# Two trunk layers on one core: layer norm in place without GpSimd, region A four units at a time, residual outputs behind later evictions

## The chip, the cores and the metric

The kernel runs on one core of one Trainium2 chip. The metric is device microseconds of a whole execution: the median of three runs before the change is 1775.16 us (1774.89 to 1776.41). The profiled execution is one more run of the same kernel; every duration below is from it.

## The reference, cut to what matters

```python
def layer(x, cond, lp, layer_idx, ctx_cache):
    sh1, sc1, g1, sh2, sc2, g2 = ...          # from silu(cond) @ w_ada + b_ada
    y, new_ctx = mixers(x * (1.0 + sc1) + sh1, lp, ...)   # w_in, conv | diff attention | MLA, w_out
    x = layer_norm(DEEPNORM_ALPHA * x + g1 * y, lp["ln1_g"], lp["ln1_b"])
    hf = x * (1.0 + sc2) + sh2
    f = (silu(hf @ lp["w_ff1"]) * (hf @ lp["w_ff3"])) @ lp["w_ff2"]
    x = layer_norm(DEEPNORM_ALPHA * x + g2 * f, lp["ln2_g"], lp["ln2_b"])
    return x, new_ctx
```

Two layers, width 1024, for 512 sample tokens and 128 prompt tokens; everything in float32, and the prompt has its own modulation vector. `layer_norm` subtracts the mean over the 1024 features, divides by the deviation, then applies a gain and a shift.

## The kernel before

**Layout.** Activations lie feature by feature: `x[k]`, k = 0 to 7, has 128 features on the partitions and 640 tokens in the columns. The columns form region A (0 to 383: 256 sample and the 128 prompt tokens) and region B (384 to 639). Every product is made as three reduced-precision products of a high and a low half (hi·hi, hi·lo, lo·hi), so the input `h[k]` of a stage is a pair (hi, lo), and a weight block ("unit", 128 output features, 1024 inputs) is DMAed to `stg` (three buffers), cast by ACT (`wu` hi, L142) and subtracted by DVE (`wu` lo, L144) into one of four `wu` buffers. PSUM tiles `mm` are two banks wide, three of them.

**Stages of a layer.** Input projections (`stage_in`), attention, output projection with first residual and norm (`stage_residual`, call it norm 1), feed-forward (`stage_ff`), whose f2 part ends in norm 2. The three norms with work behind them are norm 1 of layer 0, norm 2 of layer 0 and norm 1 of layer 1; the last norm has code of its own (`ln_last`), which stays.

**The seam of a norm.** A norm needs the sums of all eight feature tiles, so the kernel splits tokens by region: the last four output tiles of the residual stage are made for region B first and then for region A, and while region A's are made, B's norm runs; then the first four units of the next stage are multiplied for region B, while A's norm runs, and last for region A. `ln_steps` returns the steps: `stats` (matmuls of the sums with ones, then on [128, 3] tiles mean, variance and a Newton iteration for 1/deviation `ny`, L321 to 335, and `nb` = -mean·`ny`, L747), `spread` (PE transposes that spread `ny` over the partitions into `tr`, `nb` into `ac`, L753), and eight `normal(k)`: DVE a = x·G·`tr` (L767), ACT z = `ac`·G + B (L769), a += z (L770, DVE, or POOL for two tiles of region B), ACT casts h hi (L638), and lo = a - hi on DVE for region A, on POOL for region B (L639). After the last, ACT copies `ac` and `tr` to `accQ`, `accS` (L778, L779). The residual stream itself is normalised later by eight `output(k)`: three POOL operations on x (L786 to 788), then for norm 2 a DMA `xd<-x` that spills the tile (L642). `output` waits for no engine but POOL's own earlier work.

**What sets the order.** `jobs2` multiplies two units for one region and calls `hook()` after each k and unit; the tables `NEXT_FF` and `NEXT_IN` say after which hook (of 32 in region B) the next step of A's norm is issued. A scheduler then orders each engine by its own timeline; `behind(ins)` pins an instruction after another. `urgent` pins the products behind the norm's own matmuls. `PIN` keeps DVE from starting tile k before tile k - 3 is done.

**Layer 1's input stage.** After its first four units (ax0, ac0, ab0, ax1 in region order) come dk0, dq0, dk1, dq1, dv and others. dk0 and dq0 are evicted by ACT (L905, L918), rotated (DVE shuffle L826, POOL L827 for q, DVE L828, L829), split into hi and lo, moved by DMA to `ddk` and `ddq` in DRAM and loaded back as `dkp` and `dqp`; the first score matmul (L1192) needs them. The convolution of layer 1 has its first term on POOL (`cv`, L884) and the rest on DVE (L885 to 888).

Of the kernel before, what the change touches and what calls it, by code (L numbers as in the profile page):

```python
# [192 lines left out]
class Trunk:  # L193
    def __init__(self, ctx, tc, a, o):
# [160 lines left out]
    def jobs2(self, us, x, reg, nk, hooks=()):  # L355

        nc = self.nc
        c0, c1 = REG[reg]
        out = [self.mm()[:, 128:768] for _ in us]
        for k in range(nk):  # L360
            for u, ps in zip(us, out):
                for i, (pw, px) in enumerate(((0, 0), (0, 1), (1, 0))):
                    with self.behind(self.urgent):
                        self.last = nc.tensor.matmul(ps[:, c0:c1], u[:, pw, 128 * k:128 * k + 128], x(k, px)[:, c0:c1],  # L364
                                                     start=(k == 0 and i == 0), stop=(k == nk - 1 and i == 2)).ins
                self.hook()
        return out
# [311 lines left out]
    def ln_stats(self, reg, p):  # L679
# [4 lines left out]
        for i, j in enumerate(tl):  # L684
            nc.tensor.matmul(p[:, 4 * i:4 * i + 2], self.accS[:, 128 * j:128 * j + 128], self.ones2,
                             start=True, stop=True)
            self.urgent = nc.tensor.matmul(p[:, 4 * i + 2:4 * i + 4], self.accQ[:, 128 * j:128 * j + 128], self.ones2,
                                           start=True, stop=True).ins
# [47 lines left out]
    def ln_steps(self, l, s, reg):  # L736
# [4 lines left out]
        st, shift, scale, p = [], self.accQ, self.accS, self.spare  # L741

        def stats():
            y, mean = self.ln_stats(reg, p)
            nb = self.small(3, "nb")
            nt = len(TILES[reg])
            self.newton_end = nc.vector.scalar_tensor_tensor(nb[:, :nt], mean, -1.0, y[:, :nt], ALU.mult, ALU.mult).ins  # L747
            st.extend((y, nb))
# [12 lines left out]
        def normal(k):
            a, z = self.tmp("a", 1), self.tmp("z", 3)
            gb = self.gb[l + s]
            for g, b0, b1 in [(0, c0, min(c1, 256)), (1, 256, 384)] if reg == "A" else [(0, c0, c1)]:
# [1 line left out]
                with self.behind(pins.get(k - PIN)):
                    nc.vector.scalar_tensor_tensor(a[:, b0:b1], self.x[k][:, b0:b1], G, st[2][:, b0 - c0:b1 - c0],  # L767
                                                   ALU.mult, ALU.mult)
                nc.scalar.activation(z[:, b0:b1], st[3][:, b0 - c0:b1 - c0], AF.Identity, scale=G, bias=B)  # L769
            add = (nc.gpsimd if k in add_on else nc.vector).tensor_add(a[:, c0:c1], a[:, c0:c1], z[:, c0:c1]).ins  # L770
            lo = self.split_h(k, a, reg, nc.gpsimd if k in lo_on else nc.vector)
            self.pool_end = lo if k in lo_on else add if k in add_on else self.pool_end
            if PINLO and k not in lo_on:
                pins[k] = lo
            elif k not in add_on:
                pins[k] = add
            if k == NK - 1:
                nc.scalar.copy(shift[:, c0:c1], st[3])  # L778
                nc.scalar.copy(scale[:, c0:c1], st[2])  # L779
# [67 lines left out]
    def in_evac(self, l, n, ps, regs):  # L847
# [42 lines left out]
        elif n[:3] == "ckv" or n[:2] == "cq":  # L890
            raw, sq = self.t(name="raw"), self.t(name="sqr")
            nc.scalar.copy(raw, ps)
            nc.scalar.activation(sq, raw, AF.Square)
# [142 lines left out]
    def stage_in(self, l):  # L1036
# [28 lines left out]
        else:  # L1065
            us = [self.W.get((n, l)) for n in names[:nskew]]
            for regs in "BA":
                if regs == "B":
                    self.window(NEXT_IN)
                for i in range(0, nskew, 2):  # L1070
                    for n, ps in zip(names[i:i + 2], self.jobs2(us[i:i + 2], h, regs, NK)):
                        self.in_evac(l, n, ps, regs)
                        if regs == "A":
                            self.W.done()
                            self.tick()
                self.ln_inputs()
            self.ln_outputs(0 if OUTR else 1 << 30)
# [633 lines left out]
```

## Time and profile before

| | us |
|---|---|
| median of three runs | 1775.16 |
| the profiled execution's own time | 1775.88 |
| its span, first to last instruction | 1774.1 |
| PE matmul busy | 1702.8 (96%) |
| DVE busy | 1021.1 (58%) |
| ACT busy | 590.6 (33%) |
| POOL busy | 420.0 (24%) |
| mean granted TensorE clock | 0.98 of full speed |

[...] All stretches below are in us from the start of the span.

### The profile page before, as it was taken

To read this page: it belongs to the slowest core of one execution; us is meant where nothing else is said; L and a number is where in the kernel's file an instruction comes from. 1 tells how busy PE (TensorE), PEld (TensorE's weight loads), DVE (VectorE), ACT (ScalarE), POOL (GpSimd) and SP (SyncE) were. 2 spreads that over 40 slices of the span, in tenths; PEclk is the share of its full clock that TensorE was granted. 3 is DMA by queue.
4 is the path that set the end of the run, shared out by engine and by line. 5 is a ranking of instruction groups with operands and counts; after the bars stand their busy time and mean duration, and the time that the engine had idled before them with its cause. 6 is when DMAs were issued, how large, how long until landed. Compare 5 with 4: busy or idle time off the path is not lost. (4 is left out here: it accounts for less than half of the span.)

```text
span 1774.1 us, 29684 instructions
## 1 busy us (share of the span) xinstructions
PE 1702.8 (96%) x11983; PEld 1593.7 (90%) x11983; DVE 1021.1 (58%) x1824; ACT 590.6 (33%) x1010; POOL 420.0 (24%) x400
## 2 busy tenths in 40 slices
PE   8999989998999999999999899899989999999997
PEld 6998867698999999999989798677989999999997
DVE  3656776759566566856397558764682332232236
ACT  1334545525321121122243436554442212211221
POOL 0011113447701010110377111233582000000014
PEclk9999989999999999999989899899999999999998
DMA  9564584321355444544314544722122222222211
GB/s 333 196 204 140 168 250 145 109 90 48 101 149 150 149 136 140 174 130 150 93 51 166 170 113 149 210 64 84 48 75 81 72 75 81 64 79 84 68 53 59
DMA packets 100872, 217.38 MB, mean 123 GB/s; under 512 B 12160, under 2 KB 28928, under 8 KB 100736
## 3 DMA queue, kind: packets, MB, share of 16 engines
q1 hardware_dynamic: 100736, 215.50, 39.3%
q8 instruction: 94, 1.54, 0.4%
q14 instruction: 42, 0.34, 0.1%
HBM read 185.28 MB, written 30.18 MB: 121 GB/s over the span
## 5 line engine op out<-in xcount | busy, mean ns | idle before, releaser
L343 PE MATMUL mm<-h,wu 128*128 128x384 f32 (+1 forms) x4944 | 735.9, 310 | 0.2
L343 PEld LDWEIGHTS mm<-h,wu 128*128 128x128 f32 x4944 | 724.9, 189 | 6.9 <-issue 5.3
L142 ACT CAST wu<-stg 128x1024 fp32r<-128x1024 f32 (+2 forms) x200 | 201.5, 1011 | 701.3 <-issue 347.1
L144 DVE TENSOR_TENSOR wu<-stg,wu 128x1024 fp32r<-128x1024 f32 (+2 forms) x200 | 246.0, 1234 | 145.6 <-ACT wu L142 143.9
L343 PE MATMUL mm<-gh,wu 128*128 128x256 f32 (+1 forms) x1184 | 258.8, 310 | 0.0
L343 PEld LDWEIGHTS mm<-gh,wu 128*128 128x128 f32 x1184 | 198.7, 188 | 0.9 <-issue 0.6
L343 PE MATMUL mm<-gl,wu 128*128 128x384 f32 (+1 forms) x592 | 182.8, 309 | 0.0
L1196 DVE TENSOR_REDUCE nm<-mm 128x1 f32<-128x640 f32 x128 | 104.7, 818 | 54.7 <-PE mm L1192 53.8
L1545 DVE TENSOR_TENSOR gs<-gs,mm 128x640 f32<-128x640 f32 (+2 forms) x48 | 36.6, 763 | 152.7 <-PE mm L343 147.6
L653 DVE SCALAR_TENSOR_TENSOR x<-mm,ga,x 128x512 f32<-128x512 f32 x48 | 35.9, 749 | 146.2 <-PE mm L343 146.2
L672 POOL TENSOR_TENSOR accS<-x 128x640 f32<-128x640 f32 x4 | 10.0, 2490 | 443.6 <-DVE x L659 418.5
L343 PEld LDWEIGHTS mm<-gl,wu 128*128 128x128 f32 x592 | 111.4, 188 | 0.2 <-issue 0.2
L512 DVE SCALAR_TENSOR_TENSOR acc<-rawt,scT,acc 128x512 f32<-128x512 f32 x98 | 75.8, 773 | 57.8 <-DMA rawt<-in_w_ada 56.1
L364 PE MATMUL mm<-h,wu 128*128 128x384 f32 (+1 forms) x576 | 95.6, 329 | 1.0 <-DVE v L694 0.5
L364 PEld LDWEIGHTS mm<-h,wu 128*128 128x128 f32 x576 | 91.5, 206 | 3.3 <-issue 0.8
L343 PE MATMUL mm<-hi,wu 128*128 128x384 f32 (+1 forms) x400 | 89.8, 311 | 0.1
L510 POOL TENSOR_SCALAR acc<-rawt,scT 128x512 f32<-128x512 f32 x14 | 9.8, 701 | 313.0 <-PE tr L527 312.9
L1192 PE MATMUL mm<-mk,mq 96*128 96x384 f32 (+1 forms) x384 | 75.3, 337 | 5.8 <-ACT P L1207 2.3
L517 DVE SCALAR_TENSOR_TENSOR rawt<-rawt,scT 128x512 f32<-128x512 f32 x98 | 74.7, 763 | 2.1 <-POOL rawt L510 2.1
L1192 PEld LDWEIGHTS mm<-mk,mq 96*128 96x128 f32 x384 | 64.1, 201 | 12.7 <-ACT P L1207 4.9
L343 PEld LDWEIGHTS mm<-hi,wu 128*128 128x128 f32 x400 | 68.0, 188 | 2.6 <-issue 1.5
L1207 ACT ACTIVATE P<-mm,nm 128x640 f32<-128x640 f32 x56 | 44.6, 797 | 57.3 <-DVE nm L1196 45.0
(279 smaller groups left out, 2446.8 us busy)
## 6 DMA issues: line engine op xcount, KB each, us to landing
stg<-in_w_ff SPq DMA_DIRECT2D x104, 512.0 KB, 3.6
rawt<-in_w_ada SPq DMA_DIRECT2D x160, 256.0 KB, 3.0
stg<-in_w_in SPq DMA_DIRECT2D x30, 512.0 KB, 4.4
stg<-in_w_ff SPq DMA_DIRECT2D x32, 448.0 KB, 3.3
raw<-in_w_ada SPq DMA_DIRECT2D x32, 256.0 KB, 6.2
stg<-in_w_out SPq DMA_DIRECT2D x16, 512.0 KB, 4.3
mk<-kd SPq DMA_DIRECT2D x32, 240.0 KB, 5.8
mq<-qd SPq DMA_DIRECT2D x32, 192.0 KB, 5.5
```

The source lines that it names most:

```text
L142: nc.scalar.copy(u[:, 0, :ncol], t[:, :ncol])
L144: (nc.gpsimd if self.lo_pool else nc.vector).tensor_sub(u[:, 1, :ncol], t[:, :ncol], u[:, 0, :ncol].bitcast(F32))
L343: self.last = nc.tensor.matmul(out, w(k, pw), x(k, px), start=(k == 0 and i == 0), stop=(k == nk - 1 and i == 2)).ins
L364: self.last = nc.tensor.matmul(ps[:, c0:c1], u[:, pw, 128 * k:128 * k + 128], x(k, px)[:, c0:c1], start=(k == 0 and i == 0), stop=(k == nk ...
L512: nc.vector.scalar_tensor_tensor(self.acc[0], w, c[0], self.acc[0], ALU.mult, ALU.add)
L517: nc.vector.scalar_tensor_tensor(self.acc[1], w, c[1], self.acc[1], ALU.mult, ALU.add)
L653: nc.vector.scalar_tensor_tensor(lat(x), lat(ps), ga[:, 0, s, m:m + 1], lat(x), ALU.mult, ALU.add)
L672: nc.gpsimd.tensor_add(self.accS[:, c0:c1], self.first[0][:, c0:c1], x[:, c0:c1])
L1192: nc.tensor.matmul(ps[:, 128 + c0:128 + c1], q[:96, qc:qc + 128], k[:96, c0:c1], start=(i == 0), stop=(i == len(pairs) - 1))
L1196: nc.vector.tensor_reduce(nm, s, axis=AX.X, op=ALU.max, negate=True)
L1207: self.exp_end = nc.scalar.activation(P, s, AF.Exp, bias=nm, accum_out=sm).ins
L1545: nc.vector.tensor_mul(gs[:, c0:c1], gs[:, c0:c1], ps[:, c0:c1])
```

## The change

- `ln_steps`: `nb` goes, the mean itself is spread (into `ac`, as soon as it is there), then `ny`. `normal(k)` works in place: DVE x -= mean (L776 of the changed kernel), DVE x *= `ny` (L777), both with one operand in PSUM; ACT hv = G·x + B (L781, in region A in two pieces), ACT cast hi (L782), DVE lo = hv - hi (L783) for both regions. `PIN` is 2. The copies of `ac` and `tr` go.
- `output(k)` is one ACT instruction per tile and region, x = g·x + b (L790), pinned behind `out_pin`, which is set at a later eviction; three are issued per feed-forward unit pair (`OUTR`), four per unit of the input stage (`OUTI`). The spills follow.
- `jobs_by_tile` replaces `jobs2`: the two units of a pair lie in two banks of one `mm` tile; in region A all four units run at once, tile k by tile k (12 matmuls per k) for k = 0 to 5, then unit by unit for k = 6, 7 (`ENDS`). The four `wu` buffers come free only there. `hook()` is called once per k, so region B has 16 hooks.

```diff
-NEXT_FF = (10, 22, 22, 24, 24, 24, 25, 26, 27, 28)
-NEXT_IN = (10, 22, 22, 23, 24, 24, 27, 27, 29, 31)
+NEXT_FF = (7, 12, 12, 13, 14, 15, 16, 16, 16, 16)
+NEXT_IN = (7, 12, 12, 13, 14, 15, 16, 16, 16, 16)
-PIN = 3
+PIN = 2
+ENDS = 6
+OUTI = 4
...
+    def jobs_by_tile(self, us, x, reg, end=NK):
...
+        t = [self.mm() for _ in us[::2]]
+        out = [t[i // 2][:, 512 * (i % 2):512 * (i % 2) + c1 - c0] for i in range(len(us))]
+        def products(u, ps, k):
+            for i, (pw, px) in enumerate(((0, 0), (0, 1), (1, 0))):
+                with self.behind(self.urgent):
+                    self.last = nc.tensor.matmul(ps, u[:, pw, 128 * k:128 * k + 128], x(k, px)[:, c0:c1],
+                                                 start=(k == 0 and i == 0), stop=(k == NK - 1 and i == 2)).ins
+        for k in range(end):
+            for u, ps in zip(us, out):
+                products(u, ps, k)
+            self.hook()
+        for u, ps in zip(us, out):
+            for k in range(end, NK):
+                products(u, ps, k)
...
         def normal(k):
...
+            with self.behind(pins.get(k - PIN)):
+                nc.vector.tensor_sub(x[:, c0:c1], x[:, c0:c1], st[3])
+                nc.vector.tensor_mul(x[:, c0:c1], x[:, c0:c1], st[2])
             for g, b0, b1 in [(0, c0, min(c1, 256)), (1, 256, 384)] if reg == "A" else [(0, c0, c1)]:
...
+                with self.behind(casts.get(k - 2)):
+                    nc.scalar.activation(hv[:, b0:b1], x[:, b0:b1], AF.Identity, scale=G, bias=B)
+            casts[k] = self.h_end = nc.scalar.copy(hi[:, c0:c1], hv[:, c0:c1]).ins
+            pins[k] = nc.vector.tensor_sub(lo[:, c0:c1], hv[:, c0:c1], hi[:, c0:c1].bitcast(F32)).ins
...
-            with self.behind(self.pool_end if PINO else None):
-                nc.gpsimd.tensor_mul(x, x, scale[:, c0:c1])
-            nc.gpsimd.tensor_add(x, x, shift[:, c0:c1])
-            nc.gpsimd.tensor_scalar(x, x, g, b, ALU.mult, ALU.add)
+            with self.behind(self.out_pin):
+                nc.scalar.activation(x, x, AF.Identity, scale=g, bias=b)
...
+            self.window(NEXT_IN)
+            for i in range(0, nskew, 2):
+                for n, ps in zip(names[i:i + 2], self.jobs_by_tile(us[i:i + 2], h, "B")):
+                    self.in_evac(l, n, ps, "B")
+            self.ln_inputs()
+            self.window(())
+            for n, ps in zip(names[:nskew], self.jobs_by_tile(us, h, "A", ENDS)):
+                self.W.done()
+                self.in_evac(l, n, ps, "A")
+                self.tick()
...
-            self.ln_outputs(OUTR)
+            self.ln_outputs(OUTI)
```

Three places show what moves.

PE, layer 1's norm 1, region B of the first feed-forward units. Before: the spreads `tr<-first,ny` and `ac<-first,nb` stand behind 66 of the 96 products of region B (`mm<-h,wu 128x256`).

```order
L364 MATMUL mm<-h_13111,wu 128x256
L364 MATMUL mm<-h_13110,wu 128x256
L753 MATMUL tr<-first,ny 128x128 x3
L753 MATMUL ac<-first,nb 128x128 x3
L364 MATMUL mm<-h_13112,wu 128x256
```

Changed: behind 95 of the 96 (the mean has been spread behind 48), and region A's products (`128x384`) follow with two or three units in turn.

```order
L372 MATMUL mm<-h_12985,wu 128x256
L763 MATMUL tr<-first,ny 128x128 x3
L372 MATMUL mm<-h_12984,wu 128x256
L372 MATMUL mm<-h_12970,wu 128x384 x2
L372 MATMUL mm<-h_12971,wu 128x384
```

So the scales come at the end of region B's products instead of 30 products before it.

DVE, the same norm, the end of the Newton iteration of region A and the first tiles. Before:

```order
L335 SCALAR_TENSOR_TENSOR ny<-nq,ny 128x3
L1550 TENSOR_TENSOR gl<-gs,gh 128x256
L747 SCALAR_TENSOR_TENSOR nb<-mean,ny 128x3
L767 SCALAR_TENSOR_TENSOR a<-x,gb_216,tr 128x256
L767 SCALAR_TENSOR_TENSOR a<-x,gb_216,tr 128x128
L767 SCALAR_TENSOR_TENSOR a<-x,gb_216,tr 128x256
```

Changed (`h_12985` is region B's last low half, `h_12971` region A's first):

```order
L338 SCALAR_TENSOR_TENSOR ny<-nr,ny 128x3
L783 TENSOR_TENSOR h_12985<-hv,h_12984 128x256
L776 TENSOR_TENSOR x<-x,ac 128x384
L339 SCALAR_TENSOR_TENSOR nq<-ny 128x3
L776 TENSOR_TENSOR x<-x,ac 128x384
L340 TENSOR_TENSOR nq<-nq,v 128x3
L341 SCALAR_TENSOR_TENSOR ny<-nq,ny 128x3
L1547 TENSOR_TENSOR gs<-gs,mm 128x256
L777 TENSOR_TENSOR x<-x,tr 128x384 x2
L1552 TENSOR_TENSOR gl<-gs,gh 128x256
L1547 TENSOR_TENSOR gs<-gs,mm 128x256
L783 TENSOR_TENSOR h_12971<-hv,h_12970 128x384
```

Region A's first two subtractions stand inside the iteration, and B's low halves, POOL's work before, too.

SP and ACT, layer 1's input stage. SP before, with the spills `xd_96<-x` ahead of the moves of dk0 and dq0:

```order
L642 DMA xd_96<-x 128x640 x2
L273 DMA ddk_92<-hi 128x640
L273 DMA ddk_92<-lo 128x640
L273 DMA ddk_92<-hi 128x640
L642 DMA xd_96<-x 128x640 x3
L131 DMA stg<-in_w_in 128x1024
L273 DMA ddq_90<-hi 128x512 x2
L273 DMA ddq_90<-lo 128x512
```

SP changed:

```order
L279 DMA ddk_92<-hi 128x640 x2
L279 DMA ddk_92<-lo 128x640
L127 DMA stg<-in_w_in 128x1024
L279 DMA ddq_90<-hi 128x512 x2
L279 DMA ddq_90<-lo 128x512
L279 DMA dqp<-ddq_90 96x512
L279 DMA dkp<-ddk_92 96x640
```

The eight spills now stand behind the eight loads `dqp` and `dkp`, six of which and a weight load follow the last row shown.

ACT changed, between the evictions and the casts of dk0 and dq0:

```order
L908 COPY kp_9536<-mm 128x128
L138 CAST wu<-stg 128x864
L790 ACTIVATE x<-x,first 128x256 x4
L836 CAST hi<-dk 128x640
L920 ACTIVATE dq<-mm 128x640
```

Four outputs of region B now stand there, and four more ahead of the cast of dq0; before there was none.

## Rows read from the trace of the kernel before

**Rows 1.** The page, section 1: busy time of each engine, share, instructions

```profile
PE 1702.8 (96%) x11983; PEld 1593.7 (90%) x11983; DVE 1021.1 (58%) x1824; ACT 590.6 (33%) x1010; POOL 420.0 (24%) x400
```

**Rows 2.** Waits of PE: waited for, us in total, times, longest us

```profile
PE tr L753 <- DVE ny L335: 11.2, 5, 4.0
...
PE mm L1192 <- DMA dkp<-ddk: 7.3, 1, 7.3
```

**Rows 3.** Stretches: length, busy time of five engines, clock, DMA share, GB/s

```profile
415.00:437.00 22.00, 17.24 (x117) 16.24 (x116) 21.43 (x39) 8.82 (x20) 19.31 (x25) 0.84 0.15 49
429.00:436.00 7.00, 6.02 (x27) 5.62 (x28) 6.84 (x15) 3.45 (x8) 7.00 (x10) 0.51 0.00 0
903.00:926.40 23.40, 19.35 (x117) 18.09 (x117) 22.14 (x43) 10.20 (x24) 20.27 (x26) 0.78 0.21 66
1281.00:1302.00 21.00, 15.89 (x118) 15.06 (x117) 20.42 (x37) 8.99 (x20) 18.30 (x24) 0.92 0.16 51
1268.00:1281.00 13.00, 11.60 (x68) 11.31 (x67) 12.57 (x23) 8.06 (x17) 9.11 (x10) 1.00 0.27 82
978.70:985.50 6.80, 3.31 (x13) 3.34 (x14) 2.81 (x6) 1.50 (x3) 0.30 (x1) 0.50 0.91 262
```

**Rows 4.** Timeline of DVE, layer 1's first norm, region A: start, us, instruction, idle before

```profile
1285.30 2.36 DVE L144 TENSOR_TENSOR wu<-stg,wu 128x1024 fp32r<-128x1024 f32 x2
...
1294.50 0.65 DVE L335 SCALAR_TENSOR_TENSOR ny<-nq,ny 128x3 f32<-128x3 f32 x1
```

**Rows 5.** Timeline of DVE, same norm, region B

```profile
1265.33 0.17 DVE L327 TENSOR_SCALAR ny<-v 128x2 int32<-128x2 int32 x1
```

**Rows 6.** Timeline of PE, same norm: region B's scales, then region A's

```profile
1269.69 0.43 PE L753 MATMUL tr<-first,ny 128*128 128x128 f32 x2 [1.40 <-DVE ny L335]
...
1295.20 0.54 PE L753 MATMUL tr<-first,ny 128*128 128x128 f32 x3 [4.03 <-DVE ny L335]
...
1297.30 21.89 PE L364 MATMUL mm<-h,wu 128*128 128x256 f32 x126
```

**Rows 7.** Timelines of layer 1's input stage: POOL, DVE, ACT, SP's queue, PE

```profile
951.37 0.80 POOL L884 TENSOR_SCALAR cv<-upad,first 128x642 f32<-128x642 f32 x1
...
957.66 9.54 POOL L788 TENSOR_SCALAR x<-x,first 128x384 f32<-128x384 f32 x8
...
952.20 1.63 DVE L885 SCALAR_TENSOR_TENSOR cv<-upad,first,cv 128x642 f32<-128x642 f32 x1 [4.62 <-POOL cv L884]
...
957.76 0.74 DVE L826 STREAM_SHUFFLE sh<-dk 128x512 f32<-128x512 f32 x1
...
968.50 0.69 DVE L829 TENSOR_TENSOR dq<-dq,sh 128x512 f32<-128x512 f32 x1 [2.40 <-POOL sh L827]
...
961.80 0.73 ACT L834 CAST hi<-dk 128x640 fp32r<-128x640 f32 x1 [9.36 <-DVE dk L829]
962.43 0.70 ACT L918 ACTIVATE dq<-mm 128x640 f32<-128x640 f32 x1
...
971.66 0.45 SPq L273 DMA_DIRECT2D ddq<-lo  x1
...
978.02 0.32 SPq L273 DMA_DIRECT2D dqp<-ddq  x1
...
982.19 0.87 PE L1192 MATMUL mm<-dkp,dqp 96*128 96x384 f32 x2 [7.28 <-DMA dkp<-ddk]
```

**Rows 8.** Groups by line and shape, 1281 to 1319 us: DVE, then ACT

```profile
L639 DVE TENSOR_TENSOR h<-a,h 128x384 fp32r<-128x384 f32 x8 | 5.1, 637 | 0.2
L767 DVE SCALAR_TENSOR_TENSOR a<-x,gb,tr 128x256 f32<-128x256 f32 x9 | 4.2, 468 | 0.0
...
L769 ACT ACTIVATE z<-ac,gb 128x256 f32<-128x256 f32 x9 | 5.1, 566 | 4.9 <-PE ac L753 3.9 <-DVE h L639 1.0
...
L638 ACT CAST h<-a 128x384 fp32r<-128x384 f32 x8 | 4.1, 517 | 0.6 <-DVE a L770 0.6
L769 ACT ACTIVATE z<-ac,gb 128x128 f32<-128x128 f32 x8 | 3.6, 455 | 0.0
```

More of the change, by code (lines that the diff above doesn't have):

```diff
@@ L51 @@
 MODV = True
-PIN = 3
+PIN = 2
+ENDS = 6
+ACV = 2
 TABLE = True
-PINO = True
-PINLO = True
 OUTR = 3
-ADP_A = ()
-ADP_B = (5, 7)
+OUTI = 4
 ADV = 0
-ACV = 2
 HOLD = 2
@@ L163, in done, with __init__, __getitem__ @@
         self.pump()
+class Region:
+    def __init__(self, ps, c0):
+        self.ps, self.c0 = ps, c0
+    def __getitem__(self, i):
+        return self.ps[:, i[1].start - self.c0:i[1].stop - self.c0]
 class Raw:
@@ L217, in __init__ @@
         self.ada_due = []
-        self.urgent = self.pool_end = None
+        self.urgent = None
         self.window(())
@@ L353, in job @@
         return ps[:, 128:768]
-    def jobs2(self, us, x, reg, nk, hooks=()):
+    def jobs_by_tile(self, us, x, reg, end=NK):
         nc = self.nc
         c0, c1 = REG[reg]
-        out = [self.mm()[:, 128:768] for _ in us]
-        for k in range(nk):
-            for u, ps in zip(us, out):
[L362 to L367, printed above, removed]
+        t = [self.mm() for _ in us[::2]]
[6 more added lines that the diff above has]
+        for k in range(end):
+            for u, ps in zip(us, out):
+                products(u, ps, k)
[3 more added lines that the diff above has]
+                products(u, ps, k)
+        return [Region(ps, c0) for ps in out]
     def hook(self):
@@ L684, in ln_stats @@
         for i, j in enumerate(tl):
[L685 to L688, printed above, removed]
+            for o, t in enumerate((self.accS, self.accQ)):
+                self.urgent = nc.tensor.matmul(p[:, 4 * i + 2 * o:4 * i + 2 * o + 2], t[:, 128 * j:128 * j + 128],
+                                               self.ones2, start=True, stop=True).ins
         sv = p[:, :4 * nt].rearrange("p (j o) -> p o j", o=4)
@@ L740, in ln_steps @@
         c0, c1 = REG[reg]
-        st, shift, scale, p = [], self.accQ, self.accS, self.spare
+        st, p = [], self.spare
         def stats():
[L744 to L748, printed above, removed]
+            st.extend(self.ln_stats(reg, p))
         def spread():
@@ L756, in spread @@
             self.W.behind = None
-        add_on, lo_on = ((ADP_B, LOP_B) if reg == "B" else (ADP_A, LOP_A))
-        pins = {}
+        pins, casts = {}, {}
         def normal(k):
-            a, z = self.tmp("a", 1), self.tmp("z", 3)
             gb = self.gb[l + s]
+            x = self.x[k]
+            hi, lo = self.h[k]
+            hv = self.tmp("hv", 1)
+            with self.behind(pins.get(k - PIN)):
+                nc.vector.tensor_sub(x[:, c0:c1], x[:, c0:c1], st[3])
+                nc.vector.tensor_mul(x[:, c0:c1], x[:, c0:c1], st[2])
             for g, b0, b1 in [(0, c0, min(c1, 256)), (1, 256, 384)] if reg == "A" else [(0, c0, c1)]:
                 G, B = gb[:, g, 1 - s, 0, k:k + 1], gb[:, g, 1 - s, 1, k:k + 1]
[L766 to L779, printed above, removed]
+                with self.behind(casts.get(k - 2)):
+                    nc.scalar.activation(hv[:, b0:b1], x[:, b0:b1], AF.Identity, scale=G, bias=B)
+            casts[k] = self.h_end = nc.scalar.copy(hi[:, c0:c1], hv[:, c0:c1]).ins
+            pins[k] = nc.vector.tensor_sub(lo[:, c0:c1], hv[:, c0:c1], hi[:, c0:c1].bitcast(F32)).ins
         def output(k):
@@ L892, in in_evac @@
             nc.scalar.copy(raw, ps)
[L893 removed]
+            self.out_pin = nc.scalar.activation(sq, raw, AF.Square).ins
             rows = self.raws.setdefault(n[:-1], [])
@@ L1066, in stage_in @@
             us = [self.W.get((n, l)) for n in names[:nskew]]
[L1067 to L1077, printed above, removed]
+            self.window(NEXT_IN)
[8 more added lines that the diff above has]
+                self.tick()
+            self.ln_inputs()
         for n in names[nskew:]:
@@ L1580, in stage_ff @@
                         self.ada(ADA_FF)
+                    else:
+                        self.ln_outputs(OUTR)
             if pt == 2:
@@ L1586, in stage_ff @@
                     self.open_h()
+            self.ln_outputs()
             self.stage_residual(l, 1, ("f2", l, pt), f1 - f0, lambda k, p: g[k][p], pt == 2)
```

34 lines of the change are left out of this document (15 added, 19 removed).

## The prediction

> **What bounds the kernel now.** First the page: PE is busy in 96% of the span and nothing else is over 58% [rows 1], so only two things can shorten the run: time in which PE waits, and time in which it runs at its lower clock. Second the waits of PE: the longest are those for `ny` of the norms, 11.2 us over five norm regions, and one of 7.3 us for `dkp` in layer 1's input stage [rows 2]. Third the stretches round these waits, which give idle time (length less PE busy) and clock together [rows 3]. In the seam of layer 0's norm 1 PE is busy 17.24 of 22.00 us, in norm 2's 19.35 of 23.40, in layer 1's norm 1 15.89 of 21.00: 4.8, 4.1 and 5.1 us idle. The clock is 0.84, 0.78 and 0.92 there, and 0.51 from 429 to 436, right behind a wait of 4.03 us; in that stretch 6.02 us of matmuls at half clock cost 3.0 us. For the other two I take (1 - clock) × length, at most 5.1 and 1.7 us. The seams thus lose at most 7.8, 9.2 and 6.8 us, 23.8 in all.
>
> Fourth, why `ny` is late: behind two weight splits that begin at 1285.30 stand mean, variance and iteration of region A, and `ny` ends at 1295.15 [rows 4]. An operation on [128, 3] takes 0.65 us there, and 0.17 us in region B [rows 5], where POOL runs nothing; in region A it runs the outputs of region B. PE has used up the products ahead of the spread and waits 4.03 us [rows 6].
>
> **The input stage of layer 1.** POOL is in norm 2's outputs until 967.2. Its first convolution term is squeezed in at 951.37 [rows 7], so the convolution holds DVE until 957.76, when dk0, evicted 6 us before, is rotated; its hi cast at 961.80 stands on ACT in front of dq0's eviction (962.43); q's POOL multiplication waits for the last outputs, and DVE gets it at 968.50; the last move is issued at 971.66, the loads at 978.02, the score at 982.19, 7.28 us after PE was ready.
>
> With POOL empty the term starts when DVE ran dry, 4.62 us before it took the rest up at 952.20 [rows 7]. The rest of the convolution takes 5.6 us from 948.4 to 954.0 instead of 957.76: 3.8 us earlier, and the hi cast is at 958.0, the eviction of dq0 at 958.7. Shuffle, POOL multiplication (up to 2 us), add, cast and subtraction then end at about 965.2, and the last move is out at 965.5, 6.2 us earlier. If loads and score keep the distance of 10.5 us from it, the score is ready at 976.0, PE at 974.9: 1.1 us of the wait stays. If the moves land faster, now that five spills of 320 KB no longer lie just ahead of them, none stays. Four ACT outputs ahead of each cast (4 × 0.46 us) are covered: ACT is idle 9.36 us before the first [rows 7]; ahead of the second I find 1.2 us of slack, the cover that is gone first. The half clock goes with the wait: 3.31 us of matmuls at 0.50 [rows 3] cost 1.65 us. Ceiling 7.28 + 1.65 = 8.9; I take **8.4**.
>
> **The three seams.** Gone: POOL's outputs, so Newton steps cost 0.17 to 0.2 instead of 0.65 us; `nb`. Moved into the same stretch of DVE: region B's low halves (8 × 0.4). From 1285.30 I count 2.4 (two weight splits), 12 small steps of 0.2, eleven operations of 0.4 to 0.55 on tiles: `ny` at about 1294.7, 13.5 us after the stretch of region B began (about 1281.2). But the spread now stands behind 95 products of 96. The 126 products from 1297.30 (30 of 256 columns, 96 of 384) take 21.89 us [rows 6], less 1.7 for the clock, so one takes 0.117 or 0.175 us. 96 × 0.117 us, 1.5 for the sums and 0.5 for the mean's spread make 13.2 us, so PE arrives just as `ny` does: the 4.03 us and 1.0 us waits nearly go.
>
> What takes their place is that nothing covers what follows the spread: mul 0.55, ACT's pieces for k = 0 and 1, 2 × (0.57 + 0.46) less 0.1 of overlap each, 1.6, the cast 0.52 [rows 8] and handovers 0.3: **3.0 us** of idle PE before region A, and 0.3 for the first low half. In region A `PIN` = 2 makes a loop of two tiles: low half, subtraction, low half, subtraction, multiplication on DVE (5 × 0.47 as in L767, or 5 × 0.64 as in L639 [rows 8]), then 2.3 us of ACT pieces and cast. That is 4.65 to 5.5 us against 24 products × 0.175 = 4.2 us: a wait of 0.45 to 1.3 at k = 2, 4 and 6. I take the lower price, 0.5, since the rows at 0.64 ran beside POOL, which is idle now: 1.6 us. An idle 4.9 us per seam of norm 1, against 4.8 and 5.1: **no gain in waiting**. In norm 2's seam 29 products are left behind the spread, 3.4 us that cover the chain; what stays is 1.7 for a late low half of region B and 1.7 in region A, 3.4 against 4.1.
>
> So the clock decides. Behind 4.03 us idle it fell; behind the 1.40 us of region B [rows 6] it stayed at 1.00 [rows 3]; 3.0 lies between and nearer the first. I take one short stretch of 3.4 us per seam, as layer 1's norm 1 has now (0.08 × 21 × 2), 1.7 us lost. Then the seams lose 6.6, 5.1 and 6.6 us, 18.3 instead of 23.8: gain **5.5**. In the rows a cast of 384 columns from SBUF takes 0.52 us and a scaled piece of 256 from PSUM 0.57 [rows 8], so hv is priced as z was. [...]
>
> **The rest.** The four `wu` buffers come free only in the last 2.4 us of region A; the next unit needs a cast of 1.04 and a subtraction of 1.23, so I charge 0.3 us a seam, 0.9 (0 to 2). 48 ACT outputs of 0.4 to 0.55 us lie under an engine busy 33% [rows 1]; they cost nothing unless they stand ahead of an eviction PE waits for, bounded by one output each, 0.5 us at about four places. The later spills hold `x` tiles nobody rewrites before norm 1 of layer 1: nothing. Region B's seams keep their 1.40 us.
>
> Sum, from the profiled 1775.9 (0.7 over the median): 1775.9 - 8.4 - 5.5 + 0.9 = **1763 us**.
>
> **The rivals.**
> - *Seams heal.* If the loop keeps ahead (ACT and DVE overlap better than I count) and the clock stays up, seams lose only 3 us each: gain 14.8 instead of 5.5, 1754; with 1.5 us each, 1749. For it: DVE's [128, 3] steps are four times shorter. Against: the spread's place. Chance 0.17.
> - *The score wait stays.* The loads at 978 wait for moves to land beside weights at a DMA share of 0.91 [rows 3], or the outputs on ACT hold the cast; the wait keeps 4 to 7 us and the seams give 0 to 5: 1769 to 1776, about 1773 in the middle, no change. Chance 0.16.
> - *Slower: region A at half clock.* With all four units tile by tile, PE has no other work when a tile is late; each wait at k = 2, 4, 6 could keep the clock down over most of the 16.8 us. It decides from 12.9 us at half clock per seam: 6.4 lost and 4.9 idle, 34 in all, eat 23.8 plus the 7.5 net of the input stage. With all of region A down, 8.4 + 4.9 three times is 39.9, 16.1 more than now, and 1775.9 - 7.5 + 16.1 = 1784. Against: at half clock PE's pace is 8.4 us per two tiles, so the loop of 5 runs ahead and the waits end. [...] Chance 0.08.
>
> **How the numbers follow.** The forecast, 1756 to 1770, has 0.59. A measurement tells 0.2%, 3.6 us, from no change. Faster by more (under 1771.6): the forecast, the healed seams and a part of the second rival, 0.80. Same: 0.12. Slower: 0.08. The range reaches to 1750 for half of the healed case and to 1775 for most of the second.
>
> **What would show it.** Right: no PE wait on `dkp` over 2 us, score before 977; small DVE steps at 0.17 to 0.2 in the iteration of region A; no wait of PE on `ny` over 1 us, one of some 3 us on the hi cast at the first product of region A, short ones at k = 2, 4, 6; a clock under 0.95 in each seam's stretch. Wrong: seams of 31 to 33 us in all at clock 1.00 (healed); a wait on `dkp` of 4 us or more; region A longer than 25 us at clock 0.5.

## The result and the profile after

The changed kernel takes **1757.46 us** (median of four runs, 1756.95 to 1758.9) against 1775.34 of the kernel before in the same rounds (1774.89 to 1776.41): ratio **0.9897** (95% interval 0.9886 to 0.9909), 18 us less. The forecast was 1763 in a range of 1750 to 1775.

The page, section 1, of the changed kernel (busy time of each engine; compare [rows 1]): POOL lost 172 us, DVE 46, ACT gained 24, and PE's busy time hardly moved.

```profile
PE 1698.5 (97%) x11983; PEld 1589.4 (91%) x11983; DVE 975.0 (56%) x1824; ACT 614.1 (35%) x1046; POOL 247.7 (14%) x226
```

Its waits of PE (waited for, us in total, times, longest): those for `ny` and for `dkp` [rows 2] are gone; two others stand in their place.

```profile
PE mm L372 <- ACT h L782: 7.1, 6, 2.8
...
PE mm L349 <- ACT kp L908: 1.5, 1, 1.5
```

Where the span's 18.9 us went, from PE's timelines of both kernels (first and last hooked product of each seam, first `dkp` product), in us:

| stretch | before | after | gain |
|---|---|---|---|
| start to the seam of layer 0's norm 1 | 415.32 | 411.76 | 3.56 |
| that seam (192 products) | 38.44 | 37.68 | 0.76 |
| to the seam of norm 2 | 449.59 | 448.97 | 0.62 |
| that seam | 40.04 | 35.51 | 4.53 |
| its end to the first score of layer 1 | 38.80 | 33.14 | 5.66 |
| to the seam of layer 1's norm 1 | 299.02 | 294.84 | 4.18 |
| that seam | 37.64 | 37.69 | -0.05 |
| to the last matmul | 445.66 | 445.99 | -0.33 |

Three entries need a word. In the first, 1.05 us lie ahead of layer 0's first score (103.19 against 102.14), where the change touches nothing. In the first, third and sixth the residual stages are shorter by 1.5, 0.6 and 1.55 us: PE's waits for region B's `ny`, 1.38, 0.36 and 1.40 us (the last in [rows 6]), are gone. The sixth also holds what the half clock behind the old `dkp` wait cost, 1.55 us (from 982.2 to 985.5 a product of 288 columns took 0.240 us, and 0.134 at full clock behind it). What is left of the first and the sixth, some 1.0 us each, goes with half clock in the attention stages, which is not shown to come from the change: from 242 to 261 the mean clock was 0.64 before and 0.73 after, and from 1010 to 1024 it was 0.88 before, with no such stretch after.

Stretches of the changed kernel (length; busy time of PE, PEld, DVE, ACT, POOL; clock, DMA share, GB/s; compare [rows 3]): the three seams, and the stretches at half clock in the seams of norm 1 (for layer 0's, only the first of its two).

```profile
411.70:449.50 37.80, 34.72 (x212) 33.22 (x211) 24.06 (x62) 19.96 (x42) 0.00 (x0) 0.91 0.09 29
417.90:421.30 3.40, 3.40 (x19) 3.40 (x18) 3.23 (x16) 1.70 (x4) 0.00 (x0) 0.50 0.83 284
898.40:934.00 35.60, 34.21 (x211) 31.48 (x211) 24.64 (x66) 21.29 (x45) 0.00 (x0) 0.95 0.11 35
1261.90:1299.70 37.80, 34.70 (x211) 33.20 (x211) 24.06 (x62) 20.02 (x42) 0.00 (x0) 0.91 0.08 29
1267.80:1271.20 3.40, 3.40 (x18) 3.40 (x18) 3.23 (x17) 1.69 (x4) 0.00 (x0) 0.51 0.80 287
1281.50:1284.90 3.40, 3.40 (x12) 3.40 (x12) 2.34 (x6) 1.49 (x4) 0.00 (x0) 0.50 0.00 0
```

PE is idle 3.1 us in each norm 1 seam, 1.4 in norm 2's, POOL not busy at all in any. Half clock (0.50) takes 3.4 us behind the matmuls of the sums in all three seams and, in both seams of norm 1, 3.4 us behind the wait ahead of region A. In layer 1's norm 1 a product of 256 columns follows the one before it after 0.213 us there and after 0.117 at clock 1.00, one of 384 after 0.320 and 0.173; 3.4 us at half clock thus lose 1.5 us on the first kind and 1.6 on the second.

That wait, on PE's timeline (start, us, instruction, idle before) of layer 1's norm 1; compare [rows 6]:

```profile
1272.99 4.39 PE L372 MATMUL mm<-h,wu 128*128 128x256 f32 x35
1277.22 0.49 PE L763 MATMUL tr<-first,ny 128*128 128x128 f32 x3
...
1280.65 19.28 PE L372 MATMUL mm<-h,wu 128*128 128x384 f32 x96 [2.82 <-ACT h L782]
1299.76 6.45 PE L349 MATMUL mm<-h,wu 128*128 128x384 f32 x42
```

DVE's timeline of the same seam; compare [rows 4] and [rows 5]:

```profile
1269.83 0.17 DVE L333 TENSOR_SCALAR ny<-v 128x3 int32<-128x3 int32 x1
...
1273.27 0.55 DVE L776 TENSOR_TENSOR x<-x,ac 128x384 f32<-128x384 f32 x1 [1.67 <-PE ac L763]
...
1274.47 0.16 DVE L341 SCALAR_TENSOR_TENSOR ny<-nq,ny 128x3 f32<-128x3 f32 x1
...
1280.63 0.56 DVE L783 TENSOR_TENSOR h<-hv,h 128x384 fp32r<-128x384 f32 x1 [1.20 <-ACT h L782]
...
1285.71 0.56 DVE L783 TENSOR_TENSOR h<-hv,h 128x384 fp32r<-128x384 f32 x1 [1.87 <-ACT h L782]
...
1290.47 0.56 DVE L783 TENSOR_TENSOR h<-hv,h 128x384 fp32r<-128x384 f32 x1 [1.87 <-ACT h L782]
```

The iteration's small operations take 0.17 us instead of 0.65. Yet `ny` ends only at 1274.63, because the first subtraction stands in the middle of the iteration and waits 1.67 us for the mean's spread; PE spreads `ny` at 1277.22, behind 95 of 96 products (the mean's spread stands behind 60, not the 48 given above), and region A begins 2.82 us after its last cover. Low halves of tiles 0, 2 and 4 begin at 1280.63, 1285.71 and 1290.47: 4.8 us per two tiles in the steady part, with DVE idle 1.87 us of it behind ACT.

In the input stage of layer 1 (PE, then SP's queue; compare [rows 7]) the last move of dq0 goes out at 954.74 and the score starts at 967.06 without waiting; spills follow the loads.

```profile
956.77 7.27 PE L349 MATMUL mm<-h,wu 128*128 128x384 f32 x48 [1.52 <-ACT kp L908]
...
967.06 0.46 PE L1194 MATMUL mm<-dkp,dqp 96*128 96x384 f32 x2
```

```profile
954.74 0.46 SPq L279 DMA_DIRECT2D ddq<-lo  x1
958.36 0.32 SPq L279 DMA_DIRECT2D dqp<-ddq  x1
...
963.17 3.33 SPq L657 DMA_DIRECT2D xd<-x  x4
```

### The profile page after: what moved, and what is told of

It reads as the page before. It is cut to its first block, busy times and chain, and to the rows that moved or that the text cites. A ratio compares the mean times of both kernels' runs of the same rounds, so it can differ in the third digit from the quotient of the medians.

```text
span 1755.2 us, 29477 instructions
## 1 busy us (share of the span) xinstructions
PE 1698.5 (97%) x11983; PEld 1589.4 (91%) x11983; DVE 975.0 (56%) x1824; ACT 614.1 (35%) x1046; POOL 247.7 (14%) x226
## 4 chain that ended last, share of the span: by engine, by line
PE 86%; DVE 5%; ACT 3%; DMA 2%; issue 2%; POOL 0%; SPq 0%; POOLq 0%; ACTq 0%; DVEq 0%
PE mm L349 61%; PE mm L1194 4%; PE mm L372 4%; PE ac L1280 3%; PE mm L1513 3%; PE trx L1269 3%; PE mm L994 2%; PE mm L401 1%; DMA rawt<-in_w_ada 1%; ACT hv L781 1%; PE ac L476 1%; ACT wu L138 1%; DVE wu L140 1%; PE tr L449 1%; DMA mk<-kd 1%
## 5 line engine op out<-in xcount | busy, mean ns | idle before, releaser
L140 DVE TENSOR_TENSOR wu<-stg,wu 128x1024 fp32r<-128x1024 f32 (+2 forms) x200 | 239.3, 1199 | 155.9 <-ACT wu L138 153.6
L372 PEld LDWEIGHTS mm<-h,wu 128*128 128x128 f32 x576 | 92.2, 205 | 12.6 <-ACT h L782 10.2
L1194 PEld LDWEIGHTS mm<-mk,mq 96*128 96x128 f32 x384 | 63.7, 200 | 12.3 <-ACT P L1209 5.2
```

The lines of the kernel that those rows point to most:

```text
L140: (nc.gpsimd if self.lo_pool else nc.vector).tensor_sub(u[:, 1, :ncol], t[:, :ncol], u[:, 0, :ncol].bitcast(F32))
L372: self.last = nc.tensor.matmul(ps, u[:, pw, 128 * k:128 * k + 128], x(k, px)[:, c0:c1], start=(k == 0 and i == 0), stop=(k == NK - 1 and i ...
L1194: nc.tensor.matmul(ps[:, 128 + c0:128 + c1], q[:96, qc:qc + 128], k[:96, c0:c1], start=(i == 0), stop=(i == len(pairs) - 1))
```

## The experiments

All ratios are to the kernel before on the same chip and in the same rounds; times of stretches are from each run's own trace, since half clock in the attention stages differs from run to run (13.7 us in layer 0's in run 7, 6.8 in run 4, by the paces above some 3 us of a span). A part of a seam's length moves in the same way: in the changed kernel and in run 11 each seam of norm 1 holds 3.4 us at half clock behind the matmuls of the sums, worth 1.5 us (the 31 products behind them take 5.50 us in layer 1's, and 3.98 in run 2 without it); in runs 1 to 4, 8 and 9 neither does, and in runs 5, 7 and 10 only layer 1's. Differences of under 2 us between seams of two runs are therefore not put down to the edit.

**1. Outputs on POOL.** `nc.scalar.activation(x, x, Identity, scale=g, bias=b)` becomes `nc.gpsimd.tensor_scalar(x, x, g, b, mult, add)`.

> The changed kernel with the eight residual outputs of a region on POOL instead of ACT (one multiply-add per tile, at the same places behind the same evictions). Theory A (the wait for the first score in layer 1's input stage came from POOL being full): POOL's share per tile is a third of before, 0.6 to 1.3 us, so four outputs hold POOL 3 to 5 us in front of the rotation of dq0, the score comes up to 3 us later and PE waits 0 to 2.5 us for it: ratio to before 0.990 to 0.9925. Theory B (only the place of the outputs counts, not the engine): the time of the changed kernel, ratio 0.9895 to 0.990, and no wait on dkp.

Measured 0.9912 (0.9892 to 0.9933). From the second seam's end to the score 33.15 us, as in the changed kernel (33.14), with no wait on `dkp`. But the trace shows that the pin did not hold POOL: norm 2's outputs had all run by 934.1, inside the seam, so POOL was free in the input stage, and neither theory was put to the test there. The seams of norm 1 are 0.8 us shorter than the changed kernel's, less than the 1.5 us of the half clock that is missing behind their sums; norm 2's is 2.6 longer, with 6.8 instead of 3.4 us of half clock. Nor is it shown what one POOL operation of 0.67 us a tile does to the iteration: in layer 1's norm 1 region A's eight outputs ran behind it, between 1284 and 1301. Beside the two of region B that fell into it (1276.46 to 1277.61), two small DVE operations took 0.41 and 0.32 us instead of 0.16.

**2. Region A in pairs.**

```diff
-            for n, ps in zip(names[:nskew], self.jobs_by_tile(us, h, "A", ENDS)):
-                self.W.done()
+            for i in range(0, nskew, 2):
+                for n, ps in zip(names[i:i + 2], self.jobs_by_tile(us[i:i + 2], h, "A")):
+                    self.W.done()
...
```

(and the same in the feed-forward stage)

> The changed kernel with region A multiplied pair by pair (two units tile by tile, then the other two) instead of four units at once. Theory A (the chain of subtraction, multiplication, scaling, cast and low half needs 4.75 us per two tiles, as the changed kernel's DVE rows show, and only four units, 4.2 us of products, keep PE nearly busy on it): the first pair has 2.1 us of products per two tiles, so PE waits about 2.6 us three times in each of the three seams, some 8 us a seam and half clock on top, with the weights freed earlier giving nothing: 22 to 40 us slower than the changed kernel, ratio 1.002 to 1.012. Theory B (the gain of the seams is POOL's absence alone, and the number of units is of no account): within 3 us of the changed kernel, 0.988 to 0.992.

Measured 0.9917 (0.9897 to 0.9936); seams of 36.2, 35.2 and 36.2 us, followed by a new wait of 0.64 us on the next weights; the 1.5 us by which norm 1's seams are shorter than the changed kernel's are no more than the half clock missing behind their sums. Neither theory's mechanism was put to the test: the scheduler still interleaved the pairs, because both pairs' tiles were free. Region A again took 19.3 us in layer 1's norm 1.

**3. PIN = 4.** `PIN = 2` becomes `PIN = 4`.

> The changed kernel with PIN = 4 instead of 2: DVE may subtract and multiply tiles k + 2 and k + 3 while ACT scales and casts k and k + 1. Theory A (the 2.82 us wait ahead of region A is the spread's place, and the loop's 4.75 us is DVE's idle time behind ACT): the loop falls under 4.2 us and region A of each norm is set by PE, but the 2.82 us waits and the half clock behind them stay: 1 to 3 us faster than the changed kernel, ratio 0.988 to 0.9893. Theory B (the loop is covered, since PE runs at half clock behind the wait): no difference, 0.9893 to 0.9905.

Measured 0.9896 (0.9878 to 0.9913). Seams 34.98, 38.12, 34.88: the seams of norm 1 gain 2.7 and 2.8 us, of which 1.5 is the half clock missing behind their sums, norm 2's loses 2.6, where a wait of 2.50 us appeared ahead of region A. Theory A for the rest in norm 1, where the wait ahead of region A stays (2.62 us); no net gain.

**4. `ny` first.**

```diff
-            for src, ps in zip(st[:2], (self.tr(), self.ac())):
+            for src, ps in ((st[1], self.ac()), (st[0], self.tr())):
...
-            with self.behind(pins.get(k - PIN)):
+            with self.behind(pins.get(k - PIN, self.newton_end)):
...
```

> The changed kernel with the subtractions of the first tiles pinned behind the end of the Newton iteration, and the spread of ny ahead of the pinned products, so that 24 of region B's 96 products follow it. Theory A (the first subtractions stand inside the iteration on DVE and wait 1.67 us for the mean's spread, so ny is 2.6 us late, and its spread stands behind 95 products so that nothing covers multiplication, scaling and cast): the wait of 2.82 us ahead of region A falls under 1 us in both seams of norm 1 and the half clock behind it goes, 4.5 us each; waits of 0.5 us at k = 2, 4 and 6 appear in their place, 1.6 each: 4 to 8 us faster than the changed kernel, ratio 0.985 to 0.9875. Theory B (the wait moves to ny itself, which PE now reaches 2.8 us earlier): no gain, 0.989 to 0.991.

Measured **0.9854** (0.9834 to 0.9874), seams of 33.90, 33.93 and 33.88 us, no half clock in any. PE in layer 1's norm 1: `ny`'s spread follows the mean's at once, 24 products cover what comes next, and 1.31 and 0.40 us of waiting remain.

```profile
1268.20 0.49 PE L763 MATMUL ac<-first,mean 128*128 128x128 f32 x3
1268.53 0.49 PE L763 MATMUL tr<-first,ny 128*128 128x128 f32 x3
1268.78 3.08 PE L372 MATMUL mm<-h,wu 128*128 128x256 f32 x24
1273.17 4.69 PE L372 MATMUL mm<-h,wu 128*128 128x384 f32 x24 [1.31 <-ACT h L782]
1278.26 14.19 PE L372 MATMUL mm<-h,wu 128*128 128x384 f32 x72 [0.40 <-ACT h L782]
```

Theory A in direction: the wait ahead of region A falls from 2.82 to 1.31 us (it was to fall under 1), and the half clock behind it is gone. The half clock behind the sums, 1.5 us more in each norm 1 seam, is gone too, which the edit is not shown to have done. DVE's order and the spread's place change together here, so their shares are not separated. In region B's seams PE waited 1.16 and 1.18 us for `ny` again: the order that put 18 products between the mean's and `ny`'s spread is what had removed that wait.

**5. One PSUM tile per unit.** In pairs as in run 2, and `out = [self.mm()[:, :c1 - c0] for _ in us]` in `jobs_by_tile`.

> The changed kernel with one PSUM tile per unit again (three tiles in all), region A in pairs: only three of the four units can be under way at once. The run in which region A was written in pairs but kept two units per tile left PE's order and region A's 19.3 us as they were, so what allows four units at once is the shared tile. Theory A (the shared tile is what feeds PE while the chain brings a tile every 2.4 us): with three units 3.15 us of products stand against 4.75 us per two tiles, and the fourth comes after; a seam gets 3 to 8 us longer, 9 to 24 us in all, ratio 0.995 to 1.004. Theory B (the tiles are of no account): 0.9885 to 0.992.

Measured 0.9948 (0.9933 to 0.9964); seams of 38.78, 40.63 and 40.28 us. PE in region A of layer 1's norm 1:

```profile
1291.32 3.48 PE L371 MATMUL mm<-h,wu 128*128 128x384 f32 x18 [1.60 <-ACT h L781]
1296.07 3.47 PE L371 MATMUL mm<-h,wu 128*128 128x384 f32 x18 [1.27 <-ACT h L781]
1300.83 3.49 PE L371 MATMUL mm<-h,wu 128*128 128x384 f32 x18 [1.29 <-ACT h L781]
```

18 products, three units, and a wait, every 4.75 us: the loop of two tiles, made visible. Theory A: the three seams take 8.8 us more than the changed kernel's, although they hold less half clock (10.2 against 17.0 us), so the shared tile, which lets four units run at once, carries the change's gain there.

**6. The kernel before with its outputs pinned later.** Three POOL operations a tile are kept and pinned behind the evictions that the change uses.

> The kernel before with one thing of the change: its residual outputs (three POOL operations a tile, kept) come behind the later evictions, three per feed-forward pair and four per unit of the input stage. Theory A (POOL beside the Newton iteration makes DVE's small operations 0.65 instead of 0.17 us and ny 4 us late): with POOL idle there the waits of 4.03 and 2.2 us for ny go and the half clock behind them, 4 to 7 us per seam, while the input stage of layer 1 keeps its wait on dkp or gets 1 to 3 us more of it: 9 to 18 us faster than before, ratio 0.990 to 0.995. Theory B (ny is late by DVE's own load and the spread's place): seams as before, ratio 0.999 to 1.002.

Measured 1.0025 (1.0013 to 1.0038). DVE's small operations, and POOL beside them, in layer 1's norm 1:

```profile
1289.18 0.65 DVE L327 TENSOR_SCALAR ny<-v 128x3 int32<-128x3 int32 x1
```

```profile
1289.09 2.10 POOL L786 TENSOR_TENSOR x<-x,accS 128x256 f32<-128x256 f32 x3
```

0.65 us still, because the outputs still ran there, from 1282.36 on, while ACT's first gate eviction of this stage ran at 1300.19: the pin did not make POOL wait for an ACT instruction. On ACT, where the change put the outputs, the same pin does hold (the first three run at 1308.55, right behind the eviction at 1307.96). So this run says nothing on its question, and run 9 asks it again. Its input stage has a wait of 3.05 us for `kp`, which comes up again below.

**7. `ny` first for region A alone** (region B's spreads in the change's order).

> As the run with ny first, but for region A alone: region B's spreads keep the change's order. In that run region B waited 1.16 and 1.18 us for ny again, which the change had removed. Theory A (those waits come from tying region B's ny to its mean's spread): they go, and the time is 2 to 3 us under that run's, ratio 0.9835 to 0.985. Theory B (they belong to something else): as that run, 0.985 to 0.987.

Measured 0.9858 (0.984 to 0.9876). Region B's waits for `ny` are gone, as theory A has it; the total says nothing more, since 13.7 us at half clock in layer 0's attention stand against 6.8 us in run 4. Seams 33.77, 34.33, 35.34, the last with the half clock behind the sums.

**8. The same with PIN = 4.**

> The same with PIN = 4. In the run with ny first and PIN = 2 PE still waited 1.3 us ahead of region A and 0.4 us at k = 2, with clock 1.00 throughout, so the loop is now on the path. Theory A (DVE's idle time behind ACT is the loop's excess): region A follows without waits inside, 17 us, and a seam takes 32.5 to 33.5 instead of 33.9: 1 to 4 us faster than PIN = 2, ratio 0.982 to 0.984. Theory B (with PIN = 4 DVE does four subtractions and four multiplications ahead of the first low half, and the wait ahead of region A grows by what the loop gives): no difference, 0.9835 to 0.9855.

Measured 0.9881 (0.9861 to 0.99). Region A follows without waits inside, but begins late:

```profile
1280.44 18.54 PE L372 MATMUL mm<-h,wu 128*128 128x384 f32 x96 [2.23 <-ACT h L784]
```

DVE does four subtractions and four multiplications ahead of the first low half, so the wait ahead of region A goes from 0.42 to 2.23 us. Theory B, and worse.

**9. The kernel before with its outputs held back.** Ahead of each group POOL copies one column of the later eviction, so the outputs really wait for it:

```diff
+    def hold(self):
+        if self.out_src is not None:
+            d = self.small(3, "hold")
+            self.out_hold = self.nc.gpsimd.tensor_copy(d[:, :1], self.out_src).ins
+            self.out_src = None
+        return self.out_hold
...
-            with self.behind(self.pool_end if PINO else None):
+            with self.behind(self.hold()):
...
```

> The kernel before with its three POOL output operations per tile held back for real: ahead of each group POOL copies one column of the later eviction (a feed-forward gate, or kp and qp in the input stage), so the outputs cannot start before it. In the run with a pin alone they ran beside the Newton iteration as before. Theory A (POOL beside it makes ny late): small DVE operations at 0.17 us, the waits for ny ahead of region A under 1 us, seams 3 to 6 us shorter each; the input stage keeps POOL full later, so its score comes as late as before or later (0 to +4 us): 6 to 16 us faster than before, ratio 0.991 to 0.9965. Theory B (DVE's own load and the spread's place make the wait): seams within 2 us of before, ratio 0.9975 to 1.003.

Measured **0.9956** (0.9944 to 0.9969), seams of **31.06**, 35.73 and **31.11** us. DVE and PE in layer 1's norm 1:

```profile
1284.23 0.17 DVE L334 TENSOR_SCALAR ny<-v 128x3 int32<-128x3 int32 x1
...
1286.02 0.16 DVE L342 SCALAR_TENSOR_TENSOR ny<-nq,ny 128x3 f32<-128x3 f32 x1
```

```profile
1286.54 0.49 PE L760 MATMUL tr<-first,ny 128*128 128x128 f32 x3
1286.86 0.49 PE L760 MATMUL ac<-first,nb 128*128 128x128 f32 x3
1287.11 21.05 PE L371 MATMUL mm<-h,wu 128*128 128x256 f32 x126
```

The small operations take 0.16, `ny` ends at 1286.18 instead of 1295.15 [rows 4], 9.5 us into the seam instead of 13.9, and PE meets no wait: the seam is as short as its products. Theory A. The three seams gain 18.2 us, and 10.7 of them are given back between norm 2's seam and the next one: 348.5 us against 337.8 before. The first score is not late, 32.5 us behind norm 2's seam instead of 38.8. But POOL has the outputs of region A ahead of its multiplication for the rotation of dq1:

```profile
970.28 2.59 POOL L795 TENSOR_SCALAR x<-x,first 128x384 f32<-128x384 f32 x4
972.83 1.26 POOL L834 TENSOR_TENSOR sh<-sh,rope 128x512 f32<-128x512 f32 x1
```

DVE waits 11.42 us for it; its addition behind that, with POOL in the next outputs, takes 6.33 us (0.68 in the changed kernel, with POOL idle), and only then, at 980.38, comes the maximum of the first score, which its softmax needs. PE stands meanwhile:

```profile
982.17 0.90 PE L1201 MATMUL mm<-dkp,dqp 96*128 96x384 f32 x2 [15.72 <-ACT Pt L1216]
```

15.72 us of waiting, and products at half clock behind it: the nine of 288 columns from 982.87 on take 2.36 us, 0.24 us each.

**10. `ny` first for region A, and each multiplication right behind its subtraction.**

```diff
...
-                nc.vector.tensor_sub(x[:, c0:c1], x[:, c0:c1], st[3])
-                nc.vector.tensor_mul(x[:, c0:c1], x[:, c0:c1], st[2])
+                with self.behind(muls.get(k - 1)):
+                    sub = nc.vector.tensor_sub(x[:, c0:c1], x[:, c0:c1], st[3]).ins
+            with self.behind(sub):
+                muls[k] = nc.vector.tensor_mul(x[:, c0:c1], x[:, c0:c1], st[2]).ins
```

> As the run with ny first for region A (PIN = 2), with the multiplication of a tile right behind its subtraction and ahead of the next tile's, so ACT gets a tile after three DVE operations instead of five. Theory A (DVE's order holds ACT: 1.87 us of DVE idle in each loop): the loop of two tiles falls from 4.75 to about 4.0 us, under PE's 4.2, the first cast of region A comes 0.5 us earlier, and the waits of 0.4 us in region A go: seams of 32 to 33.5 us, 1 to 5 us faster than that run in all, ratio to before 0.983 to 0.9855. Theory B (the loop is set by ACT's two pieces and cast, 2.8 us per two tiles plus the handovers): no difference, 0.985 to 0.987.

Measured **0.9826** (0.981 to 0.9842): 1744.27 us. The three seams (columns as above), and DVE's low halves of tiles 0, 2 and 4 in layer 1's norm 1:

```profile
417.30:448.30 31.00, 30.68 (x212) 30.09 (x211) 24.39 (x60) 21.46 (x43) 0.00 (x0) 1.00 0.11 35
897.00:929.90 32.90, 32.46 (x212) 31.81 (x211) 24.71 (x65) 22.58 (x45) 0.00 (x0) 0.95 0.12 35
1258.50:1291.00 32.50, 32.17 (x212) 31.59 (x211) 24.42 (x60) 21.39 (x43) 0.00 (x0) 0.95 0.11 33
```

```profile
1274.12 0.56 DVE L787 TENSOR_TENSOR h<-hv,h 128x384 fp32r<-128x384 f32 x1 [0.34 <-ACT h L786]
...
1277.84 0.55 DVE L787 TENSOR_TENSOR h<-hv,h 128x384 fp32r<-128x384 f32 x1
...
1281.05 0.56 DVE L787 TENSOR_TENSOR h<-hv,h 128x384 fp32r<-128x384 f32 x1
```

The loop falls to 3.7 and 3.2 us, under PE's 4.2 (24 products of 0.173 us); PE is idle 0.3 to 0.4 us in a whole seam. Theory A, and the best kernel of the study. The clock of 0.95 in the last two seams is the half clock behind the sums, and PE's wait of 1.52 us for `kp` in the input stage, absent in runs 4 and 7, is there again.

**11. The changed kernel again,** in the rounds of runs 9 and 10.

> The changed kernel as it is, on the same chip and in the same rounds as the two runs beside it, to compare them: ratio 0.989 to 0.991; waits of 2.8 us ahead of region A in both seams of norm 1 and of 1.5 us on kp in the input stage again, and half clock behind the first.

Measured 0.9901 (0.9886 to 0.9916), 1758.31 us, seams of 37.68, 34.79 and 37.70, the wait of 2.82 us ahead of region A and the one of 1.5 on kp: as expected. Run 10 is 14 us faster beside it.

## Why the prediction came out as it did

**The seams: right in the sum, partly by luck.** The prediction had them lose 6.6, 5.1 and 6.6 us against an ideal of 31, a gain of 5.5; they took 37.68, 35.51 and 37.69, a gain of 5.24. Idle ahead of region A: 3.0 forecast, 2.82 measured. Loop of two tiles: 4.65 to 5.5 forecast, 4.8 measured. "No gain in waiting, so the clock decides" did not hold as reasoned, though norm 1's seams are about as long as before: their idle time fell to 3.1 us, where 4.9 was forecast, and 3.1 us were lost to half clock (1.5 and 1.6), where 1.7 was forecast. The two errors nearly cancel, and that is luck. The prediction charged half clock with half of its time, 3.0 us for 6.02, 1.7 for 3.4 and 1.65 for 3.31; no run shows that a product takes twice as long there: it took 1.82 to 1.85 times as long (0.213 us against 0.117, 0.320 against 0.173). The forecast had waits at k = 2, 4, 6 and one stretch of half clock; the trace has two stretches and, with PE at half clock behind the wait, no waits of over 0.4 us in region A. The second stretch, behind the matmuls of the sums, was not forecast, and in runs 1 and 2 it did not come. In norm 2's seam 1.4 us of idle time stand against 3.4 forecast; there the prediction counted 29 products behind the spread, and the trace has 21, which cover all but 0.73 us.

**The input stage: right, with one wait missed.** Forecast 8.4; measured 5.66 + 1.55 = 7.2. The score's wait went wholly (1.1 was to stay): the last move went out 12.3 us ahead of the score. The difference is mostly a new wait of 1.52 us from 955.25 on: dq1's first product starts at 956.77, as ACT ends the copy `kp` in the eviction of dk1. In runs 4 and 7 the wait is gone and the stretch takes 31.36 us instead of 33.14. That the change makes four PSUM tiles instead of eight ahead of dq1 does not explain it: runs 4 and 7 make four and have no such wait, run 6 makes eight and waits 3.05 us. What decides it stays open.

**"Region B's seams keep their 1.40 us": wrong,** and the largest term missed: the three residual stages are 3.7 us shorter. I looked at region B's DVE rows, found no POOL beside the iteration's first part, and left the order of PE alone, though the change splits the two spreads for region B too. Runs 4 and 7 show the cause: with `ny`'s spread directly behind the mean's the wait in norm 1 is 1.16 and 1.18 us, with 18 products between them none.

**The tail of 0.9 us: wrong.** From the end of layer 0's norm 1 seam to its next residual stage it is 423.0 us in both kernels (453.76 to 876.77, 449.44 to 872.44), and no wait on weights appears; a wait of 0.64 us shows in run 2, where the first two weights come free with the first pair.

The sum: 8.4 + 5.5 - 0.9 = 13.0 forecast; 7.2 + 5.2 + 3.7 + 0, together 16.1 from the change's parts, and the rest up to 18.9 in spans is the start (1.05) and half clock in the attention stages, which also differs between the changed kernel's two traces. So the forecast fell 5 us short, most of it the term of region B, and the time stayed inside the range.

**On why the kernel before lost time in its seams** the prediction said that POOL's operations slow the iteration; run 9 shows it, with the rest of that kernel kept: 38.44 and 37.64 us fall to 31.06 and 31.11. So the change's in-place form was not needed to heal norm 1's seams, and with its own order did not. What it gives is an input stage without POOL's outputs: from norm 2's seam to the next it takes 328.0 us against 337.8 before, and the kernel before with held outputs 348.5. Not every DVE instruction is slower beside POOL: L767, with one operand in PSUM, takes 0.468 us beside POOL's outputs [rows 8] and 0.474 with them held back in run 9, while the low half, with both operands in SBUF, takes 0.637 [rows 8] and 0.551. Run 9's groups from 1276 to 1309 us:

```profile
L646 DVE TENSOR_TENSOR h<-a,h 128x384 fp32r<-128x384 f32 x8 | 4.4, 551 | 0.2
...
L774 DVE SCALAR_TENSOR_TENSOR a<-x,gb,tr 128x256 f32<-128x256 f32 x9 | 4.3, 474 | 0.4 <-PE tr L760 0.4
```

`ny`'s operations take 0.65 against 0.16 us, the first one, which reads one tile alone, as much longer as those that read two (`ny<-v`, 0.65 in run 6, 0.17 in run 9). No run shows what decides which instruction is slowed.

hv was priced as z, though no row had its form. ACT's groups by shape of layer 1's norm 1 of the changed kernel (1277 to 1300 us):

```profile
L781 ACT ACTIVATE hv<-x,gb 128x256 f32<-128x256 f32 x8 | 4.7, 594 | 6.3 <-DVE x L777 6.2
L781 ACT ACTIVATE hv<-x,gb 128x128 f32<-128x128 f32 x8 | 3.8, 480 | 0.0
```

0.594 and 0.480 us against z's 0.566 and 0.455 [rows 8]: dearer by 0.03 us a piece.

The rival of region A at half clock did not come: at half clock the loop runs ahead, as argued, though by less than forecast: 24 products take 7.7 us there at 0.320 each, not 8.4, against a loop of 4.8. Behind the 2.82 us waits the clock fell each time, behind 1.31 us in run 4 it did not, behind 2.23 us in run 8 once of two.

Open: how much of the input stage's gain is ACT and how much the single operation (run 1 moved the engine, and its outputs ran earlier than pinned), and what decides on the half clock behind the sums.

## What to carry to other kernels

An engine off the critical path can still set it: what three lazy POOL operations a tile cost in the seams was not their time. Beside them the nine tiny DVE operations of the iteration took 5.6 us in layer 1's norm 1, and 1.5 us with them held back (0.65 and 0.16 us for most), and PE waited 4.03 us for the result [rows 6]. When a chain ends in a broadcast through PE, put the broadcast as early in PE's order as its input allows and leave independent products behind it, and give each engine of a two-engine loop the shortest run of instructions that releases the other: together that was worth 14 us beyond the change (run 10 against run 11). A scheduling pin behind an ACT instruction did not make POOL wait (in run 6 outputs from 1282.36 on, the eviction at 1300.19); look in the trace whether a pin held.

## What was not expected of the hardware

Behind the sums of a norm (12 matmuls of two columns, 1.6 us, hardly any idle time) the clock fell to 0.50 for 3.4 us in all three seams of the changed kernel, in norm 1's with PE busy throughout, and in norm 1's again in run 11; in runs 1 and 2, with the same order there, it did not.
